# Six of the second layer's twelve modulation steps, moved from the first layer to the place between the layers

## The chip, the cores and the metric

The kernel runs on one core of one Trainium2 chip. The metric is device time in microseconds. A core has TensorE (PE, matmuls), VectorE (DVE), ScalarE (ACT), GpSimd (POOL) and SyncE (SP, which issues most DMAs); they run side by side and wait for each other by semaphores.

## The reference

Two layers of a hybrid backbone block on 512 latent and 256 context tokens, 1024 wide. What matters here is the modulation at the head of each layer and where its parts are used:

```
for l in range(DEPTH):
    sh1, sc1, g1, sh2, sc2, g2 = split(silu(c) @ w_mod[l] + b_mod[l], 6)
    modc = split(silu(c_ctx) @ w_mod[l] + b_mod[l], 6)
    h = modulate(rms_norm(x, norm1_g[l]), sh1, sc1)
    hc = modulate(rms_norm(xc, norm1_g[l]), modc[0], modc[1])
    p_* = split(h @ w_in[l]), and of hc likewise
    mixed = concat(pooling, GQA, hyena, MLA) @ w_out[l]
    x_new = x + g1 * mixed
    x = x_new + g2 * expert_choice_ffn(modulate(rms_norm(x_new, norm2_g[l]), sh2, sc2))
```

`c` and `c_ctx` don't depend on the tokens, so a layer's modulation can be computed at any time before its norm. The first two of the six parts are needed by the layer's first norm, the others from the output projection on.

## The kernel before, in words

The modulation of a layer (`modulation`, L354) is twelve steps of 512 columns. A step loads two weight halves of 1 MB (`wmod[l, j, kh]`) through `load` (L239) into the ring `ringt` of three slots, on SP's queue. It has 16 matmuls of 32x512 in four column groups side by side (L367), a copy on ScalarE (`part`, L371), four transposes (L375), and a sum and the bias on VectorE (L377, L378). After the twelfth step the table `modT` is transposed and written to memory (L381 to L384, `mrow`). It is a generator: each `yield` is a place where other work can be written in between.

The second layer's modulation is such a generator, `self.side` (L316), advanced by ticks while the first layer's projection (`project_in`) and its MLA attention are written. A scheduler then orders the instructions of each engine. So the steps lie on TensorE between other matmuls, and their weights in SP's queue between other loads.

The end of layer 0 is its mixture of experts, 16 experts whose weights of 1 MB come through the same SP queue; each expert's rows are scattered back to `xs` by GpSimd (L1601). Between the layers (`layer`, L666 to L676) the tables of layer 1 are loaded, `row_loads` (L733) loads six tiles of 128 token rows (`xrow`) from `xs`, which must wait for the last scatters, and `norm_rows` computes each row's scale: a square with its sum on ScalarE (L745), root and reciprocal (L725, L726), a diagonal matrix `diag` on VectorE (L749). Then layer 1 begins: `norm1` multiplies rows by `diag` (L763), which transposes and scales them, and splits the result into a high part on ScalarE (`hT`, L766) and a low part on VectorE and GpSimd (L769 to L773). The projection's first matmuls are those of L797. Its weights (`win`) also come through `ringt`.

Of the kernel before, what the change touches and what calls it, by code (L numbers as in the profile page):

```python
# [10 lines left out]
F32 = mybir.dt.float32  # L11
F32R = mybir.dt.float32r
U32 = mybir.dt.uint32
AF = mybir.ActivationFunctionType
# [13 lines left out]
GW = [sum(b - a for a, b in g) for g in GROUPS]  # L28
# [147 lines left out]

SLOTS = ([0, 1, 4, 2, 5, 3], 5, 4), ([0, 1, 2, 7, 8, 3, 4, 5, 6], 6, 4)
EARLY = 3, 9
LATE_STEPS = ((1, 0), (1, 2), (2, 0), (2, 2))

SCALE_BY = dict(g="vvpppv", m="vvpvpp")
# [24 lines left out]
class Block:  # L206
# [50 lines left out]
    def run(self):  # L257
        nc, I = self.nc, self.I
        c = self.const
        self.cst = c.tile([128, I["cst"].shape[1]], F32, name="cst")  # L260
        nc.sync.dma_start(self.cst, I["cst"])
        self.ident = self.cst[:, 0:128]
        self.sel16 = self.cst[:, 128:144]
        self.off = self.cst[:, 144:146]
        self.flip = [self.cst[:64, 146:274], self.cst[:32, 274:402]]
        self.half = self.cst[:, 402:404]
        self.tok = self.cst[:, 404:408]
        self.ones = c.tile([128, 1], F32, name="ones")
        nc.vector.memset(self.ones, 1.0)
        self.eps = c.tile([128, 1], F32, name="eps")  # L270
        nc.vector.memset(self.eps, EPS)
        d = self.dram
        self.xs = [d.tile([n, D], F32, name=f"xs{i}") for i, n in enumerate((SEQ, CTX))]
        self.xh = [d.tile([n, D], F32, name=f"xh{i}") for i, n in enumerate((SEQ, CTX))]
        self.spec = {(l, s): d.tile([2, 128, 2 if s == "l" else 1, 2, 2, 256], F32, name=f"spec{l}{s}")
                     for l in range(2) for s in ("l", "c") if (l, s) != (1, "c")}
        self.sqn = {k: c.tile([128, 4], F32, name=f"sqn{k[0]}{k[1]}") for k in self.spec}
        self.mrow = [d.tile([48, 2, 128], F32, name=f"mrow{l}") for l in range(2)]
        cT = c.tile([128, 8, 2], F32, name="cT")
        nc.sync.dma_start(cT, I["cT"].rearrange("p (k s) -> p k s", s=2))  # L280
        tables = self.open_layer(0)
        self.lay0 = self.lay
        self.scT = self.lay.tile([128, 8, 32], F32, name="scT")
        nc.vector.memset(self.scT, 0.0)
        nc.scalar.activation(self.scT[:, :, 0:2], cT, AF.Silu)
        self.small, self.modT = {}, {}
        self.load_small(0)
        npg, self.fcg = self.pool("norm"), self.pool("filtc")
        np_ = npg.__enter__()
        self.fc = self.fcg.__enter__()  # L290
        with self.pool("filt", side="right") as p:
            scr = dict(sp=[p.tile([128, 1024], F32, name=f"fsp{i}") for i in range(4)][::-1])
            self.filter_loads(p)
            self.filter_mlp(p, scr["sp"][3][:, :NT])
            p.tile([128, 2048], F32, name="spare")
            for k, w, n in (("od", 512, 2), ("acc", 1024, 1), ("s", 1024, 1)):
                scr[k] = [p.tile([128, w], F32, name=f"f{k}{i}") for i in range(n)]
            self.tabs["l"] = p.tile([128, 2, 2, 2, 256], F32, name="fdftl")
            scr["EO"] = [p.tile([128, 4096], F32, name="fEO")]
            scr["z"] = [self.fws]  # L300
            first = []
            for i in range(8):
                own = self.layt[:, 2048 * i - 6144:2048 * i - 4096] if i in (3, 4) else None
                first.append(self.load(I["wmod"][0, i // 2, i % 2], own=own))
                if i == 2:
                    nc.sync.dma_start(self.tabs["l"], I["fdftl"].rearrange("p (x r b f) -> p x r b f", x=2, r=2, b=2))
                if i == 4:
                    rows = self.row_loads(0, np_)
            mod = self.modulation(0, first)
            for _ in range(8):  # L310
                next(mod)
            for t, src in tables:
                nc.sync.dma_start(t, src)
            xh = self.norm_rows(np_, rows)
            self.filters(scr, "l")
        self.side = chain(mod, self.modulation(1))  # L316
        for l in range(DEPTH):
            npg, xh = self.layer(l, npg, xh) or (None, None)

# [31 lines left out]
        return self.small[l][:, a:b]  # L351


    def modulation(self, l, first=()):  # L354

        nc = self.nc
        if l not in self.small:
            self.load_small(l)
        mod = self.const.tile([128, 96], F32, name="modT", tag="modT", bufs=2)
        self.modT[l] = mod  # L360
        bm = self.sm(l, "b_mod")
        for j in range(12):
            pt = self.ps1()
            for kh in range(2):
                w = first.pop(0) if first else self.load(self.I["wmod"][l, j, kh])
                for kk in range(4):
                    nc.tensor.matmul(pt[32 * kk:32 * kk + 32, :], self.scT[:, 4 * kh + kk, :],  # L367
                                     w[:, 512 * kk:512 * kk + 512], start=kh == 0, stop=kh == 1,
                                     tile_position=(0, 32 * kk))
            part = self.lay0.tile([128, 512], F32, name="part", tag="part", bufs=1)  # L370
            nc.scalar.activation(part, pt, AF.Copy)  # L371
            yield
            pm = self.ps1()
            for q in range(4):
                nc.tensor.transpose(pm[:, 128 * q:128 * q + 128], part[:, 128 * q:128 * q + 128], self.ident)  # L375
            m = mod[:, 8 * j:8 * j + 8].rearrange("p (q s) -> p q s", s=2)
            nc.vector.tensor_reduce(m, pm.rearrange("p (q k s) -> p q s k", q=4, k=4)[:, :, 0:2], axis=AX.X, op=OP.add)  # L377
            nc.vector.tensor_tensor(m, m, bm[:, 4 * j:4 * j + 4][:, :, None].to_broadcast([128, 4, 2]), op=OP.add)  # L378
            yield
        pr = self.ps1()  # L380
        nc.tensor.transpose(pr[:96, :128], mod, self.ident)  # L381
        row = self.lay0.tile([96, 128], F32, name="mrow", tag="mrow", bufs=1)
        nc.vector.tensor_copy(row, pr[:96, :128])
        nc.gpsimd.dma_start(self.mrow[l].rearrange("n s d -> (n s) d"), row)  # L384
        self.dump(f"mod{l}", mod)
# [161 lines left out]
    def layer(self, l, npg, xh):  # L547
# [28 lines left out]
        with ExitStack() as rows_stack:  # L576
            cvg = self.pool("cv")
            with self.pool("hT", side="right") as hp:
                hT = [hp.tile([128, 8, NT], F32R, name=f"hT{i}") for i in range(2)]
                self.norm1(l, hT, xh, A1, B1)  # L580
                if not l:
                    g = self.G.rearrange("p b w -> p (b w)")
                    od = self.fc.tile([128, 512], F32, name="fod")
                    scr = {k: [self.fc.tile([128, w], F32, name="f" + k)] for k, w in (("s", 1024), ("sp", 1024), ("z", 512))}
                    self.filters(dict(scr, od=[od], EO=[g[:, 0:2048]], acc=[g[:, 2048:3072]]), "c")
                    self.fcg.__exit__(None, None, None)
                self.conv_tables(l, last)
                self.gain_tables(l)
                npg.__exit__(None, None, None)
                rows = rows_stack.enter_context(self.pool("rows"))  # L590
                self.MQ = rows.tile([128, 6, 384], F32, name="rowsMQ")
                self.MK = rows.tile([128, 6, 384], F32, name="rowsMK")
                self.MV = rows.tile([128, 6, 256], F32, name="rowsMV")
                self.rsq = rows.tile([128, 6, 12], F32, name="rsq")
                self.cv = cvg.__enter__().tile([128, 6, wid], F32, name="cv")
                self.project_in(l, hT, last, side)
# [70 lines left out]
        nxt = None  # L667
        if not last:
            tables = self.open_layer(l + 1)
            npg = self.pool("norm")  # L670
            np_ = npg.__enter__()
            rows = self.row_loads(l + 1, np_)
            for t, src in tables:
                nc.sync.dma_start(t, src)
            nxt = npg, self.norm_rows(np_, rows)
        r3g.__exit__(None, None, None)  # L676
        return nxt

# [75 lines left out]
    def norm1(self, l, hT, xh, A1, B1):  # L754
        nc, p = self.nc, self.npool
        for s, b0, nb in ((0, 0, 4), (1, 4, 2)):
            o = 128 * b0
            w = 128 * nb
            for k in range(8):
                pt = self.ps1()  # L760
                for i in range(nb):
                    x, d = xh[b0 + i]
# [12 lines left out]
    def project_in(self, l, hT, last, side):  # L775
# [3 lines left out]
        wp, rp = wpg.__enter__(), rpg.__enter__()  # L779

        def split_group(g):
            w = self.load(self.I[f"win{g}"][l], 8 * GW[g])
            n = GW[g]
            hi, lo = [], []
            for k in range(8):
# [919 lines left out]
```

## Time and profile before

| | us |
|---|---|
| median of 3 runs | 1486.69 (1483.56 to 1487.9) |
| the profiled execution's own time | 1484.3 |
| its span in the trace | 1482.4 |

The mean granted clock of TensorE over the span is 0.952 of full speed. Durations are read from the profiled execution, whose span is 1.9 us shorter than its time; rows are in microseconds from the span's start, mean durations in ns where a view says so. SPq is SP's issuing sequencer.

### The profile page before, as it was taken

What the parts mean: (1) busy time and instruction counts of PE and PEld (TensorE: products, weight loads), DVE (VectorE), ACT (ScalarE), POOL (GpSimd) and SP (SyncE); (2) the same over time, 40 slices, a digit from 0 to 9 for tenths busy, and PEclk for the clock granted to TensorE, in tenths of its full rate; (3) what the DMA queues carried; (4) which work ended last, traced back from release to release, by engine and by line L of the source; (5) the groups of instructions that cost most, each with busy time, mean ns of one, the idle gap of its engine ahead of it and who ended that gap; (6) DMA issues with size and microseconds to landing.
All of it is one profiled execution on the core that took longest, in us unless ns stands there. A gap on an engine that the chain in (4) does not pass through costs nothing.

```text
span 1482.4 us, 23909 instructions
## 1 busy us (share of the span) xinstructions
PE 1345.9 (91%) x9457; PEld 888.8 (60%) x9457; DVE 684.3 (46%) x1831; ACT 507.1 (34%) x1238; POOL 341.9 (23%) x360
## 2 busy tenths in 40 slices
PE   6999999888899998999999968988899974998896
PEld 2577787777678895444444437977778961332221
DVE  4656364687663547122222227585787452221111
ACT  4545333435564433111111136544357430111000
POOL 1510141254210115121222132042521011111101
PEclk9989999999899998999999989999999986999998
DMA  9546746011265139899999980123100858999996
GB/s 386 220 159 243 278 156 245 31 58 43 79 264 170 58 128 350 341 395 392 396 392 398 386 283 5 61 83 139 57 30 3 350 203 326 406 393 409 405 402 215
DMA packets 72737, 345.96 MB, mean 233 GB/s; under 512 B 7105, under 2 KB 23105, under 8 KB 38322
## 3 DMA queue, kind: packets, MB, share of 16 engines
q1 hardware_dynamic: 57488, 305.24, 52.3%
q0 software_dynamic: 13104, 32.19, 8.0%
q10 hardware_dynamic: 2034, 7.00, 1.2%
q8 instruction: 75, 1.23, 0.3%
q14 instruction: 36, 0.29, 0.1%
HBM read 317.70 MB, written 26.71 MB: 232 GB/s over the span
## 4 chain that ended last, share of the span: by engine, by line
PE 74%; DVE 9%; DMA 9%; ACT 3%; issue 3%; POOL 1%; POOLq 0%; ACTq 0%; DVEq 0%; SPq 0%
PE b L1622 13%; PE b L808 7%; PE b L1655 6%; PE b L1633 4%; PE b L1116 3%; PE b L367 3%; PE b L797 3%; PE b L798 3%; PE b L799 3%; PE b L1064 3%; DMA ring<-wu 3%; PE b L1304 3%; PE b L1306 3%; PE b L1305 3%; PE b L1139 3%
## 5 line engine op out<-in xcount | busy, mean ns | idle before, releaser
L1622 PE MATMUL b<-ring,xg 128*64 128x512 f32 x824 | 222.4, 618 | 13.5 <-DMA ring<-wu 10.6
L1622 PEld LDWEIGHTS b<-ring,xg 128*64 128x64 f32 x824 | 66.9, 141 | 130.5 <-issue 103.1
L1608 ACT ACTIVATE sgl<-b 64x512 f32<-64x512 f32 x32 | 18.9, 591 | 345.9 <-PE b L1622 345.9
L1655 PE MATMUL b<-ring,hTm 128*64 128x512 f32 x464 | 110.9, 605 | 2.0 <-DVE hTm L1649 1.3
L797 PE MATMUL b<-whi,hT 128*128 128x256 f32 (+1 forms) x352 | 103.1, 294 | 0.3 <-DVE h L769 0.3
L798 PE MATMUL b<-wlo,hT 128*128 128x256 f32 (+1 forms) x352 | 100.3, 285 | 0.0
L799 PE MATMUL b<-whi,hT 128*128 128x256 f32 (+1 forms) x352 | 99.9, 284 | 0.0
L1116 PE MATMUL b<-kop,qop 96*128 96x512 f32 (+3 forms) x360 | 86.1, 370 | 13.5 <-ACT P L1121 10.8
L808 PE MATMUL b<-hT,whi 128*128 128x512 f32 (+1 forms) x384 | 96.3, 357 | 1.5 <-DVE cv L864 1.3
L721 DVE TENSOR_TENSOR wlo<-ringt,whi 128x256 fp32r<-128x256 f32 (+1 forms) x192 | 83.0, 474 | 30.1 <-ACT whi L718 29.7
L1649 DVE COPY hTm<-b 128x384 f32<-128x384 f32 (+1 forms) x32 | 15.7, 491 | 164.0 <-PE b L1646 98.3
L718 ACT ACTIVATE whi<-ringt 128x256 fp32r<-128x256 f32 (+1 forms) x192 | 67.5, 404 | 47.6 <-PE b L808 22.4
L1601 POOL DMA_INDIRECT xs<-y,sidx x32 | 50.2, 1568 | 135.0 <-DVE y L1599 131.5
L1121 ACT ACTIVATE P<-b,nm 128x768 f32<-128x768 f32 (+1 forms) x80 | 65.4, 818 | 38.9 <-DVE nm L1118 37.2
L1118 DVE TENSOR_REDUCE nm<-b 128x1 f32<-128x768 f32 (+1 forms) x80 | 67.1, 845 | 23.1 <-PE b L1116 22.4
L797 PEld LDWEIGHTS b<-whi,hT 128*128 128x128 f32 x352 | 68.4, 195 | 12.3 <-issue 3.7
L1116 PEld LDWEIGHTS b<-kop,qop 96*128 96x128 f32 (+1 forms) x360 | 58.5, 201 | 25.2 <-ACT P L1121 14.0
L808 PEld LDWEIGHTS b<-hT,whi 128*128 128x128 f32 x384 | 63.2, 188 | 15.3 <-ACT oT L1263 2.1
L1304 PE MATMUL b<-whi,oT 128*128 128x256 f32 x240 | 71.3, 299 | 0.0
L798 PEld LDWEIGHTS b<-wlo,hT 128*128 128x128 f32 x352 | 68.7, 195 | 3.2 <-issue 2.5
L1655 PEld LDWEIGHTS b<-ring,hTm 128*64 128x64 f32 x464 | 32.7, 138 | 60.9 <-issue 57.4
L1144 ACT ACTIVATE PT<-b 128x384 f32<-128x384 f32 (+1 forms) x140 | 57.3, 448 | 34.4 <-PE b L1139 33.5
(398 smaller groups left out, 2881.1 us busy)
## 6 DMA issues: line engine op xcount, KB each, us to landing
ring<-wd SPq DMA_DIRECT2D x58, 1024.0 KB
ring<-wu SPq DMA_DIRECT2D x53, 1024.0 KB
ring<-wg SPq DMA_DIRECT2D x50, 1024.0 KB
ringt<-wmod SPq DMA_DIRECT2D x46, 1024.0 KB
ringt<-win SPq DMA_DIRECT2D x14, 1024.0 KB
ringt<-wg SPq DMA_DIRECT2D x14, 1024.0 KB
ringt<-wu SPq DMA_DIRECT2D x11, 1024.0 KB
ringt<-wout SPq DMA_DIRECT2D x8, 1024.0 KB
```

What stands on the lines that cost most here:

```text
L718: nc.scalar.activation(hi, src, AF.Copy)
L721: nc.vector.tensor_tensor(lo, src, hi.bitcast(F32), op=OP.subtract)
L797: nc.tensor.matmul(pt[:, :n], hT[0][:, k, t], hi[k], start=k == 0, stop=False)
L798: nc.tensor.matmul(pt[:, :n], hT[0][:, k, t], lo[k], start=False, stop=False)
L799: nc.tensor.matmul(pt[:, :n], hT[1][:, k, t], hi[k], start=False, stop=k == 7)
L808: nc.tensor.matmul(pt[:, a:b], w[k][:, cs], hT[h][:, k, a:b], start=first and k == 0, stop=end and k == 7)
L1116: nc.tensor.matmul(S[:, s:e], q[a][:K, c], k[b][:K, k0 + s:k0 + e], start=y == 0, stop=y == len(terms) - 1)
L1118: nc.vector.tensor_reduce(nm, S[:, :n], axis=AX.X, op=OP.max, negate=True)
L1121: nc.scalar.activation(P[:, :n], S[:, :n], AF.Exp, bias=nm, accum_out=sm)
L1304: nc.tensor.matmul(pt[:, :256], oT[0][k][:, t], hi[k], start=k == 0, stop=False)
L1622: nc.tensor.matmul(pa[64 * j:64 * j + 64], X[:, k, o:o + 64], w[k // 4][:, c], start=k == 0, stop=k == 7, tile_position=(0, 64 * j))
L1655: nc.tensor.matmul(py[64 * j:64 * j + 64], hT[:, f], wd[f // 2][:, d:d + 512], start=f == 0, stop=f == 3, tile_position=(0, 64 * j))
```

## The change

`SPLIT = 6`: the generator of layer 1 in layer 0 runs its steps 0 to 5 alone. A second one, for steps 6 to 11, is made between the layers, with a `scT` of its own (`scT1`, the activated `c`), a pool `wm` of three buffers and two slots of `ringt` for its twelve weight halves. The first projection weight (`win2`, `self.win0`) is loaded ahead of them. `in_order` makes TensorE keep the written order from there to the end of `norm1`. Steps 6 to 8 stand ahead of the norm, 9 to 11 in it. No arithmetic is added or left out.

```diff
-        self.side = chain(mod, self.modulation(1))
+        self.side = chain(mod, self.modulation(1, j1=SPLIT))
...
             tables = self.open_layer(l + 1)
-            npg = self.pool("norm")
+            npg, wmg = self.pool("norm"), self.pool("wm")
             np_ = npg.__enter__()
-            rows = self.row_loads(l + 1, np_)
+            scT = np_.tile([128, 8, 32], F32, name="scT1")
+            nc.gpsimd.memset(scT, 0.0)
+            nc.scalar.activation(scT[:, :, 0:2], self.cT, AF.Silu)
+            slots = [("wm", 3)] * 12
+            slots[3] = slots[4] = ("ringt", self.RING)
+            wm, todo = wmg.__enter__(), [(j, h) for j in range(SPLIT, 12) for h in range(2)]
+            ready = []
+
+            def fetch(n=1):
+                for _ in range(n):
+                    if todo:
+                        j, h = todo.pop(0)
+                        tag, bufs = slots.pop(0)
+                        w = (wm if tag == "wm" else self.ring).tile([128, 2048], F32, name=tag, tag=tag, bufs=bufs)
+                        nc.sync.dma_start(w, I["wmod"][l + 1, j, h])
+                        ready.append(w)
+
+            def take():
+                if not ready:
+                    fetch()
+                return ready.pop(0)
+
+            self.win0 = self.load(I["win2"][l + 1], 8 * GW[2])
+            fetch(5)
+            mod = self.modulation(l + 1, [take] * 12, SPLIT, 12, np_, scT)
             for t, src in tables:
                 nc.sync.dma_start(t, src)
+            self.between = self.in_order()
+            self.between.__enter__()
+            next(mod)
+            fetch(2)
+            next(mod)
+            next(mod)
+            rows = self.row_loads(l + 1, np_)
+            fetch(1)
+            next(mod)
+            next(mod)
             nxt = npg, self.norm_rows(np_, rows)
+            next(mod)
+            self.late_mod = mod, fetch, wmg
...
             for k in range(8):
+                if l and (k in (1, 2, 4, 5) if not s else k in (1, 2)):
+                    next(self.late_mod[0], None)
+                    if k in (1, 4):
+                        self.late_mod[1](2)
                 pt = self.ps1()
```

On SP, the issues between layer 0's last expert weight (`ring<-wd`) and layer 1's projection weights, before:

```order
L1556 DMA ring_7921<-wd 128x2048
L239 DMA ringt<-win 128x1280
L239 DMA ringt<-win 128x2048 x2
L733 DMA xrow<-xs_75 128x1024 x4
L733 DMA xrow<-xs_76 128x1024 x2
L239 DMA ringt<-win 128x2048 x5
```

and in the changed kernel, at the same place:

```order
L1608 DMA ring_7784<-wd 128x2048
L241 DMA ringt<-win 128x1280
L698 DMA ringt<-wmod 128x2048 x2
L698 DMA wm<-wmod 128x2048 x6
L241 DMA ringt<-win 128x2048 x2
L698 DMA wm<-wmod 128x2048
L781 DMA xrow<-xs_75 128x1024 x4
L781 DMA xrow<-xs_76 128x1024 x2
L241 DMA ringt<-win 128x2048
L698 DMA wm<-wmod 128x2048 x3
L241 DMA ringt<-win 128x2048 x4
```

Nine `wmod` loads now stand ahead of the token rows `xrow`, and three behind them.

On TensorE, the same place: the last expert's final matmuls (`hTm`) and the beginning of layer 1's norm (`diag,xrow`), before:

```order
L1663 MATMUL b_8188<-ring_7919,hTm 32x256 x8
L1663 MATMUL b_8188<-ring_7921,hTm 32x256 x8
L763 MATMUL b_8306<-diag,xrow 128x128
L763 MATMUL b_8315<-diag,xrow 128x128
L763 MATMUL b_8324<-diag,xrow 128x128
L763 MATMUL b_8333<-diag,xrow 128x128
L763 MATMUL b_8306<-diag,xrow 128x128
```

and in the changed kernel (`wm,scT` and `ringt,scT` are a step's matmuls, `cst,part` its transposes):

```order
L1715 MATMUL b_8051<-ring_7784,hTm 32x256 x8
L372 MATMUL b_8106<-wm,scT_8084 32x512 x8
L380 MATMUL b_8121<-cst,part 128x128 x4
L372 MATMUL b_8128<-wm,scT_8084 32x512 x4
L372 MATMUL b_8128<-ringt,scT_8084 32x512 x4
L380 MATMUL b_8153<-cst,part 128x128 x4
L372 MATMUL b_8160<-ringt,scT_8084 32x512 x4
L372 MATMUL b_8160<-wm,scT_8084 32x512 x4
L380 MATMUL b_8219<-cst,part 128x128 x4
L815 MATMUL b_8247<-diag,xrow 128x128 x4
L372 MATMUL b_8256<-wm,scT_8084 32x512 x8
L815 MATMUL b_8271<-diag,xrow 128x128 x4
```

Steps 6 to 8 stand ahead of the norm, step 9 behind its first group of columns. The norm's groups are now written one after the other, where before the first four were filled row by row. (One matmul of a step in the program is two in the trace: x8 here is its 16 there.)

## Rows read from the trace of the kernel before

**Rows 1.** The page, part 4: the chain that ended last, share of the span by engine.
```profile
PE 74%; DVE 9%; DMA 9%; ACT 3%; issue 3%; POOL 1%; POOLq 0%; ACTq 0%; DVEq 0%; SPq 0%
```

**Rows 2.** The chain in 238 to 264: start, us, what.
```profile
249.25 0.44 PE b L375 x4
249.68 1.85 PE b L367 x16
```

**Rows 3.** The lines of 400 to 456: busy us, mean ns, idle before.
```profile
L371 ACT ACTIVATE part<-b 128x512 f32<-128x512 f32 x5 | 3.0, 597 | 4.5 <-PE b L367 4.5
```

**Rows 4.** The chain in 398 to 457: start, us, what.
```profile
400.60 1.85 PE b L367 x16
...
406.62 0.59 PE b L375 x4
...
434.92 1.00 PE b L367 x8
...
437.51 0.99 PE b L367 x8
...
456.30 0.26 PE b L381
456.58 0.30 DVE mrow L383
```

**Rows 5.** Windows: us, busy of PE, PEld, DVE, ACT, POOL; clock, DMA share, GB/s.
```profile
410.00:420.00 10.00, 9.64 (x104) 7.33 (x102) 5.82 (x15) 7.82 (x21) 0.48 (x1) 1.00 0.47 173
440.00:450.00 10.00, 10.00 (x95) 7.54 (x94) 5.84 (x14) 7.34 (x19) 1.81 (x2) 1.00 0.43 140
1120.00:1130.00 10.00, 10.00 (x98) 8.79 (x97) 7.50 (x16) 8.38 (x22) 1.21 (x2) 1.00 0.01 2
```

**Rows 6.** TensorE's waits in 384 to 456: us in total, times, longest.
```profile
PE b L1139 <- ACT PT L1144: 0.4, 1, 0.4
```

**Rows 7.** Windows between the layers, columns as in rows 5.
```profile
844.00:852.00 8.00, 8.00 (x61) 2.97 (x59) 1.70 (x8) 0.00 (x0) 3.10 (x2) 1.00 1.01 409
...
862.00:866.00 4.00, 3.30 (x44) 1.61 (x42) 1.79 (x3) 0.34 (x1) 3.84 (x15) 1.00 1.02 428
866.00:870.00 4.00, 4.00 (x32) 1.55 (x32) 0.66 (x1) 0.00 (x0) 2.73 (x2) 1.00 0.77 146
870.00:874.00 4.00, 1.17 (x24) 0.42 (x16) 2.54 (x10) 1.69 (x7) 2.48 (x2) 1.00 0.49 44
...
878.00:882.00 4.00, 0.00 (x0) 0.00 (x0) 0.00 (x0) 1.78 (x3) 0.00 (x0) 0.50 0.94 347
882.00:886.00 4.00, 2.41 (x11) 2.44 (x12) 1.14 (x6) 3.92 (x9) 0.00 (x0) 0.50 1.03 406
886.00:892.00 6.00, 4.37 (x25) 4.17 (x24) 2.69 (x8) 5.94 (x12) 0.00 (x0) 0.73 0.42 173
892.00:898.00 6.00, 4.96 (x40) 4.44 (x39) 6.00 (x11) 4.29 (x8) 3.93 (x3) 1.00 0.00 0
898.00:904.00 6.00, 4.18 (x28) 3.48 (x29) 6.00 (x12) 3.52 (x7) 3.21 (x4) 1.00 0.00 0
```

**Rows 8.** SP's rows in 850 to 890: first issue, us, what.
```profile
857.29 2.05 SPq L239 DMA_DIRECT2D ringt<-win  x3
876.25 3.08 SPq L733 DMA_DIRECT2D xrow<-xs  x6
```

**Rows 9.** ScalarE's rows in 868 to 904: start, us, what.
```profile
880.20 1.06 ACT L745 ACTIVATE junk<-xrow 128x1024 f32<-128x1024 f32 x1 [8.39 <-issue]
...
889.44 2.78 ACT L766 ACTIVATE hT<-b,B,A 128x512 fp32r<-128x512 f32 x4
```

**Rows 10.** TensorE's rows in 868 to 904.
```profile
883.59 6.48 PE L763 MATMUL b<-diag,xrow 128*128 128x128 f32 x32 [12.42 <-DVE diag L749]
...
903.50 0.34 PE L797 MATMUL b<-whi,hT 128*128 128x160 f32 x1 [0.26 <-DVE h L769]
```

**Rows 11.** The line of a step's matmuls: duration in ns, min/median/max.
```profile
L367 PE MATMUL b<-ringt,scT x368: 592/592/1062, 12.2 to 448.0; 128*32 128x512 f32 x184
```

More of the change, by code (lines that the diff above doesn't have):

```diff
@@ L178 @@
 EARLY = 3, 9
+SPLIT = 6
 LATE_STEPS = ((1, 0), (1, 2), (2, 0), (2, 2))
@@ L278, in run @@
         self.mrow = [d.tile([48, 2, 128], F32, name=f"mrow{l}") for l in range(2)]
-        cT = c.tile([128, 8, 2], F32, name="cT")
+        cT = self.cT = c.tile([128, 8, 2], F32, name="cT")
         nc.sync.dma_start(cT, I["cT"].rearrange("p (k s) -> p k s", s=2))
@@ L351, in sm, with modulation @@
         return self.small[l][:, a:b]
-    def modulation(self, l, first=()):
+    def modulation(self, l, first=(), j0=0, j1=12, p=None, scT=None):
         nc = self.nc
@@ L358, in modulation @@
             self.load_small(l)
-        mod = self.const.tile([128, 96], F32, name="modT", tag="modT", bufs=2)
-        self.modT[l] = mod
+        if not j0:
+            self.modT[l] = self.const.tile([128, 96], F32, name="modT", tag="modT", bufs=2)
+        mod = self.modT[l]
         bm = self.sm(l, "b_mod")
-        for j in range(12):
+        p, scT = p or self.lay0, self.scT if scT is None else scT
+        for j in range(j0, j1):
             pt = self.ps1()
@@ L365, in modulation @@
                 w = first.pop(0) if first else self.load(self.I["wmod"][l, j, kh])
+                w = w() if callable(w) else w
                 for kk in range(4):
-                    nc.tensor.matmul(pt[32 * kk:32 * kk + 32, :], self.scT[:, 4 * kh + kk, :],
+                    nc.tensor.matmul(pt[32 * kk:32 * kk + 32, :], scT[:, 4 * kh + kk, :],
                                      w[:, 512 * kk:512 * kk + 512], start=kh == 0, stop=kh == 1,
                                      tile_position=(0, 32 * kk))
-            part = self.lay0.tile([128, 512], F32, name="part", tag="part", bufs=1)
+            part = p.tile([128, 512], F32, name="part", tag="part", bufs=1)
             nc.scalar.activation(part, pt, AF.Copy)
@@ L379, in modulation @@
             yield
+        if j1 < 12:
+            return
         pr = self.ps1()
         nc.tensor.transpose(pr[:96, :128], mod, self.ident)
-        row = self.lay0.tile([96, 128], F32, name="mrow", tag="mrow", bufs=1)
+        row = p.tile([96, 128], F32, name="mrow", tag="mrow", bufs=1)
         nc.vector.tensor_copy(row, pr[:96, :128])
@@ L580, in layer @@
                 self.norm1(l, hT, xh, A1, B1)
+                if l:
+                    for _ in self.late_mod[0]:
+                        pass
+                    self.between.__exit__(None, None, None)
+                    self.late_mod[2].__exit__(None, None, None)
                 if not l:
@@ L781, in split_group @@
         def split_group(g):
-            w = self.load(self.I[f"win{g}"][l], 8 * GW[g])
+            w = self.win0 if l and g == 2 else self.load(self.I[f"win{g}"][l], 8 * GW[g])
             n = GW[g]
```

## The prediction

> **What bounds the kernel now.** I read five views in order: the chain that ended last, the stretches in which the six moved steps run, TensorE's waits there, the stretch between the layers, and the rows of DMA issues, ScalarE and TensorE in it. The chain is TensorE's for 74% of the span [rows 1], so TensorE time taken off is a gain wherever TensorE has no gaps, and time put where TensorE waits costs nothing by itself.
>
> The moved steps first. Only one of the six lies beside the first layer's projection: its 16 matmuls start at 249.68 [rows 2]. The other five lie in the MLA attention of layer 0: five ScalarE copies, one for each step, in 400 to 456 [rows 3]. In that attention TensorE is busy 9.64 and 10.00 us of 10, at full clock [rows 5], and it waits 0.4 us in 72 [rows 6]. The reader is to see that the weights are always there and that ScalarE (7.82 of 10) and VectorE (5.84) have room: what leaves TensorE here comes off the end. Layer 1's same attention, which has no modulation in it, also stands at 10.00 of 10 with ScalarE at 8.38 [rows 5], so I expect the thinned attention to stay with TensorE.
>
> Between the layers it is the other way. After the last expert TensorE waits 12.4 us for the first `diag` [rows 10]. Until 866 the expert weights and the projection's first weights come at 409 to 428 GB/s [rows 7]; then the queue is nearly empty, because the six token rows (`xrow`) are issued only at 876.25, after the last expert's scatters [rows 8]. The first row reaches ScalarE at 880.20 [rows 9], the norm's matmuls run from 883.59 and the projection begins at 903.50 [rows 10]. In that norm ScalarE is busy 5.94 of 6 us from 886 to 892, and VectorE 6.00 of 6 from 892 to 904 [rows 7]: it is a chain over three engines, and TensorE has gaps in it.
>
> **The gain in layer 0.** Per step the chain has 16 matmuls, 1.85 us, and four transposes, 0.59 us [rows 4]. The five steps in the attention: four times 1.85, once 1.00 + 0.99 (in two halves), and five times 0.59: 9.39 + 2.95 = 12.3 us. After the last one stand the transposition of the whole table, 0.26, and the copy on which the attention then waits, 0.30: 0.6 us [rows 4]. The projection's step is 1.85 us and 0.44 us of transposes (taken from those of the step ahead of it) [rows 2]: 2.3 us. Sum 15.2 us. I take 15.0, since single gaps may reopen. The lower bound is 12: it lets a fifth be lost to ScalarE and VectorE, which have 2 to 4 us of every 10 left. The twelve weight loads that leave layer 0's queue count nothing: TensorE waited for no weight there [rows 6].
>
> **The price between the layers.** Steps 6 to 8 stand before the norm, where TensorE has 12.4 us of nothing to do, so their matmuls are hidden by that wait, and so are the memset and the activation that rebuild `scT`: ScalarE is idle in 844 to 852 [rows 7]. What isn't hidden is their weights. In SP's order nine of the twelve 1 MB loads stand before `xrow`, and the projection's `win` loads with them, as now. The three loads that were issued at 857.29 [rows 8] keep the queue busy until about 867.4 (146 GB/s over 866 to 870 is 1.4 us at 428 [rows 7]). After the change two `wmod` loads stand at the place of two of these, and what follows is nine loads more: 9 x 1.049 MB at 409 GB/s is 23.1 us, to 890.5. The first row, 0.52 MB, is then in at 891.8. Before, 3.95 us passed from its issue to ScalarE's start (876.25 to 880.20), 1.3 of them transfer; the issue now lies behind the queue, and I leave 0.8 for the receipt: 892.6 instead of 880.2, **12.4 us later**. At 428 GB/s it would be 10.5; at the 347 of 878 to 882 [rows 7] it would be 16.5. Behind `xrow` on SP stand one `win` load, the last three `wmod` loads and the other `win` loads; the first two projection groups have theirs by then.
>
> Next, three steps stand inside the norm. They are 3 x (1.85 + 0.59) = 7.3 us of TensorE. [...] So I double the first: 2.4 us more, 9.8 in all. In 886 to 904 TensorE has 1.6 + 1.0 + 1.8 = 4.4 us free [rows 7]. If these gaps take the work, 5.3 us remain, **which I add**. The lower bound is the three ScalarE copies alone, 1.8 us; the upper is 9.8, nothing hidden. TensorE's order also turns from row by row to group by group: the first group now needs four rows' `diag`. Its copy to `hT` came only after all six rows' squares anyway (889.44 [rows 9]), so I count nothing for it.
>
> [...]
>
> **The sum**: -15.0 + 12.4 + 5.3 = +2.7 us on the profiled execution's 1484.3: 1487.0. That execution stands 2.4 under the runs' median of 1486.7, so I name **1489.4 us**. A measurement of this kernel tells about 0.3%, 4.5 us, from no change.
>
> **The rivals.**
> A. My forecast, with its own range from the bounds that lie together: 1484 to 1494. Chance 0.45.
> B. Slower: the norm is stretched by whole steps. The last three loads are issued only when step 9 frees their buffers, behind the rows; each norm group behind a waiting step waits too, since TensorE keeps the written order. Then the inserted steps cost 9.8 instead of 5.3, and one late load of 2.6 us shows: +9.8 in all, 1496. For it: TensorE's order is strict, and ScalarE is at 5.94 of 6. Against it: the norm lasts 20 us, in which three loads are 7.7. It decides as soon as the inserted steps cost over 7.1. Chance 0.33.
> C. Faster: the rows aren't held by the queue. They can be issued when step 8 has freed its buffer: its weights are the fourth of the nine loads, in at 867.4 + 4 x 2.56 = 877.6, so near 878.5, 2.3 later than now. If their packets then pass the `wmod` loads that are queued, the price is 2.3 + 5.3 = 7.6 and the time -7.4: 1479. For it: the rows are 3.1 MB of the 15 that are in the queue. Against it: the loads issued at 857.29 were still in the queue at 867, so what is issued next stands behind ten us of work now, too. Chance 0.14.
> D. Layer 0 gives back only part: the attention is then held by its softmax chain, and half of the 12.3 us is lost: +8.9, 1496. For it: of every 10 us 7.8 would be left to TensorE (12.3 of some 56 are gone), and 7.2 to ScalarE (7.82 less a copy of 0.6). Against it: layer 1's attention [rows 5]. Chance 0.08.
>
> [...]
>
> **How the numbers follow.** A's own range crosses 4.5 us either way a little: of its 0.45, 0.38 is within, 0.05 above, 0.02 below. B gives 0.28 slower and 0.05 within, C 0.12 faster and 0.02 within, D 0.08 slower. So faster 0.14, same 0.45, slower 0.41. The range 1480 to 1499 holds A, B and D's midpoint and leaves out most of C and the far ends: about 2 in 10.
>
> **What would show it.** In the changed profile: no row of the step in 400 to 440 and an attention about 12 us shorter; DMA near full share from 862 to 895 of the present time scale where it is now 0.49 at 870 to 874; ScalarE's first square about 12 us later, counted from the last expert matmul; the time from the first norm matmul to the projection 4 to 8 us longer than 19.9. I am wrong if the first square is less than 5 us later, if the norm takes over 28 us, or if the attention stays as long as it is.

## The result, and the profile after

The changed kernel takes 1502.2 us (median of 7 runs, 1492.1 to 1505.5) against 1485.3 (7 runs): the ratio is 1.010, 95% interval 1.0074 to 1.0127. It is slower, by about three times what a measurement tells from no change, and above the range that was given. The profiled execution took 1503.0 us, its span 1501.1.

TensorE's share of the chain fell and DMA's rose, against [rows 1]. The page's part 4 after the change:

```profile
PE 71%; DMA 13%; DVE 9%; ACT 4%; issue 2%; POOL 1%; POOLq 0%; ACTq 0%; SPq 0%; DVEq 0%
```

In the attention of layer 0 the steps are gone and TensorE is as full as in [rows 5], with ScalarE a little fuller. Windows after, columns as there:

```profile
400.00:410.00 10.00, 10.00 (x76) 8.60 (x77) 7.60 (x18) 8.05 (x23) 1.82 (x2) 1.00 0.01 2
440.00:450.00 10.00, 10.00 (x118) 8.53 (x118) 5.16 (x15) 8.00 (x28) 2.66 (x7) 1.00 0.18 54
```

Between the layers, TensorE's rows after, which answer to [rows 10]. The last expert's matmuls end at 863.88:

```profile
863.90 1.06 PE L372 MATMUL b<-wm,scT 128*32 128x512 f32 x8
867.47 1.53 PE L372 MATMUL b<-wm,scT 128*32 128x512 f32 x8 [2.50 <-DMA wm<-wmod]
...
878.52 0.65 PE L380 MATMUL b<-cst,part 128*128 128x128 f32 x4 [0.78 <-ACT part L376]
892.55 0.77 PE L815 MATMUL b<-diag,xrow 128*128 128x128 f32 x2 [13.38 <-DVE diag L797]
...
897.25 3.64 PE L372 MATMUL b<-wm,scT 128*32 128x512 f32 x16
...
904.72 1.92 PE L372 MATMUL b<-wm,scT 128*32 128x512 f32 x16
...
911.22 1.92 PE L372 MATMUL b<-wm,scT 128*32 128x512 f32 x16
...
918.74 0.34 PE L849 MATMUL b<-whi,hT 128*128 128x160 f32 x1
```

Steps 6 to 8 end at 879.2 and TensorE then waits 13.4 us, a little longer than the 12.4 without them: the gap was not filled, it was moved behind the steps. Why is seen in the chain of the same stretch (start, us, what), where two DMA pieces take 21 us of the 62 from 857 to 919:

```profile
857.21 10.21 DMA wm<-wmod
...
878.19 10.81 DMA xrow<-xs
889.10 1.15 ACT junk L793 x2
```

and in the windows, which answer to [rows 7]: the queue is full throughout, and in the middle it moves 357 GB/s, not 409.

```profile
854.00:864.00 10.00, 9.28 (x96) 3.86 (x96) 2.59 (x5) 0.00 (x0) 6.68 (x17) 1.00 1.02 412
864.00:878.00 14.00, 9.77 (x56) 2.45 (x55) 1.39 (x7) 1.32 (x3) 3.13 (x2) 0.76 1.05 357
878.00:890.00 12.00, 0.65 (x4) 0.42 (x4) 2.24 (x10) 3.17 (x10) 0.00 (x0) 0.65 1.02 413
```

**Stage by stage.** I cut each trace at the first or last matmul of a stage: the end of the projection (L808), the last hyena matmul (L1218), the first of the router (L1339), the first and the last of the experts (L1622, L1663), the first and last of the norm (L763), and the same in layer 1. The first column is before, in us; the others are differences to it in the profile of each kernel (the experiments are told below).

| stage | before | changed | e5 | e1 | e2 | e3 | e4 | e6 | e7 | e8 | e9 | e10 |
|---|---|---|---|---|---|---|---|---|---|---|---|---|
| layer 0 hyena, first attention | 102.7 | +5.4 | +3.5 | +1.9 | +0.4 | +0.4 | +3.5 | +4.3 | +3.4 | 0.0 | +3.5 | -0.2 |
| to the attention's end | 80.8 | -14.2 | -12.6 | -14.2 | -1.7 | -14.2 | -12.6 | -14.2 | -12.6 | -7.7 | -12.6 | -12.6 |
| output projection, routing | 133.8 | +2.4 | +4.4 | +4.1 | -0.2 | +3.9 | +4.4 | +4.2 | +4.4 | +9.9 | +4.4 | +4.1 |
| experts | 276.7 | +0.3 | -0.9 | -0.9 | +0.4 | -0.9 | -0.9 | -0.9 | -0.9 | -0.5 | -0.9 | -0.9 |
| wait for the norm | 12.4 | +16.3 | +16.3 | -0.9 | +16.7 | +16.2 | +12.8 | +15.7 | +4.5 | +9.4 | -1.7 | -1.1 |
| norm | 19.7 | +6.1 | +6.5 | -1.0 | +5.9 | +6.0 | +9.2 | 0.0 | +1.8 | -0.8 | -1.0 | -0.8 |
| layer 1 projection | 122.4 | +1.6 | 0.0 | -1.4 | 0.0 | +1.6 | 0.0 | -1.4 | +2.4 | 0.0 | +0.4 | -0.5 |
| layer 1 hyena, first attention | 64.0 | +4.3 | +4.4 | -1.0 | +2.5 | -2.0 | +2.5 | -1.0 | +0.3 | +0.7 | +7.7 | +9.0 |
| to the attention's end | 64.5 | -0.6 | -0.6 | 0.0 | -0.7 | 0.0 | -0.6 | 0.0 | +0.2 | 0.0 | +6.1 | +2.7 |

Ahead of the first stage the code is that of before, but for the projection's step where SPLIT is 6, and it ends between 272.5 and 282.1 us in these profiles (276.3 on average in the seven without that step, 279.1 in the five with it). A step of 2.3 us can't be read from such a spread. Nor do differences of about 1 us in a stage mean much: from the experts to layer 1's hyena e1 runs the work of before, and its stages are 0.9 to 1.4 shorter than in the one profile of before, whose 1484.3 us stand 3 above the later medians of before (1481.3 and 1481.5). So the ratios are the measure of a kernel, the stages that of a place.

### The profile page after: what moved, and what is told of

Its sections match the earlier page's. It is cut to its first block, busy times and chain, and to the rows that moved or that the text cites. A ratio compares the mean times of both kernels' runs of the same rounds, so it can differ in the third digit from the quotient of the medians.

```text
span 1501.1 us, 23922 instructions
## 1 busy us (share of the span) xinstructions
PE 1347.3 (90%) x9457; PEld 890.7 (59%) x9457; DVE 679.9 (45%) x1831; ACT 507.8 (34%) x1239; POOL 342.1 (23%) x361
## 4 chain that ended last, share of the span: by engine, by line
PE 71%; DMA 13%; DVE 9%; ACT 4%; issue 2%; POOL 1%; POOLq 0%; ACTq 0%; SPq 0%; DVEq 0%
PE b L1674 11%; PE b L860 7%; PE b L1707 5%; PE b L1685 4%; DMA ring<-wg 4%; DMA ring<-wu 4%; PE b L1168 3%; PE b L1116 3%; PE b L849 3%; PE b L1191 3%; PE b L372 3%; PE b L850 3%; PE b L851 3%; PE b L1356 2%; PE b L1357 2%; PE b L1358 2%
## 5 line engine op out<-in xcount | busy, mean ns | idle before, releaser
L1674 PE MATMUL b<-ring,xg 128*64 128x512 f32 x824 | 216.4, 600 | 16.2 <-DMA ring<-wu 12.3
L1168 PE MATMUL b<-kop,qop 96*128 96x512 f32 (+3 forms) x360 | 84.8, 365 | 13.1 <-ACT P L1173 10.5
L1701 DVE COPY hTm<-b 128x384 f32<-128x384 f32 (+1 forms) x32 | 15.7, 490 | 159.1 <-PE b L1698 98.2
L849 PEld LDWEIGHTS b<-whi,hT 128*128 128x128 f32 x352 | 68.3, 195 | 12.2 <-issue 3.7
L860 PEld LDWEIGHTS b<-hT,whi 128*128 128x128 f32 x384 | 63.9, 190 | 14.3 <-issue 2.7
L1168 PEld LDWEIGHTS b<-kop,qop 96*128 96x128 f32 (+1 forms) x360 | 57.8, 198 | 22.8 <-ACT P L1173 13.6
L851 PEld LDWEIGHTS b<-whi,hT 128*128 128x128 f32 x352 | 68.5, 195 | 0.8 <-issue 0.8
```

What stands on the lines that cost most here:

```text
L849: nc.tensor.matmul(pt[:, :n], hT[0][:, k, t], hi[k], start=k == 0, stop=False)
L851: nc.tensor.matmul(pt[:, :n], hT[1][:, k, t], hi[k], start=False, stop=k == 7)
L860: nc.tensor.matmul(pt[:, a:b], w[k][:, cs], hT[h][:, k, a:b], start=first and k == 0, stop=end and k == 7)
L1168: nc.tensor.matmul(S[:, s:e], q[a][:K, c], k[b][:K, k0 + s:k0 + e], start=y == 0, stop=y == len(terms) - 1)
L1674: nc.tensor.matmul(pa[64 * j:64 * j + 64], X[:, k, o:o + 64], w[k // 4][:, c], start=k == 0, stop=k == 7, tile_position=(0, 64 * j))
```

## The experiments

**e1: the layer 0 part alone.** Against the changed kernel:

```diff
         if j1 < 12:
-            return
+            nc.gpsimd.memset(mod[:, 8 * j1:], 0.0)
...
-            scT = np_.tile([128, 8, 32], F32, name="scT1")
...
             self.win0 = self.load(I["win2"][l + 1], 8 * GW[2])
-            fetch(5)
-            mod = self.modulation(l + 1, [take] * 12, SPLIT, 12, np_, scT)
+            rows = self.row_loads(l + 1, np_)
...
```

> Steps 6 to 11 are left out altogether (their columns of the table are zeros), so this is the layer 0 part of the change alone. Forecast: TensorE's time comes off the end, 13 to 15 us faster than before, near 1471. Rival 1, the attention can't use the time that is freed: 9 to 10 us faster, near 1476, as the changed kernel's layer 0 gave. Rival 2, the changed kernel's layer 0 lost some 5 us because the scheduler wrote the hyena stage in another order: here that order is nearly the one of before, so 13 to 15 us faster as well, and the stretch from the projection to the end of the hyena is as long as before within 2 us.

Measured: ratio 0.9936 (0.9923 to 0.9949), 9.5 us. The 13 to 15 that were expected did not come: the amount is rival 1's, but not the place. The attention itself gives the whole 14.2: TensorE waits 0.2 us in 400 to 448, so rival D is out, and so is rival 1 as it was put. But 4.1 us are given back in the routing and 1.9 in the hyena, whose order here is neither that of before nor that of the changed kernel.

**e2: the price alone.**

```diff
-        self.side = chain(mod, self.modulation(1, j1=SPLIT))
+        self.side = chain(mod, self.modulation(1, end=False))
...
-        if j1 < 12:
+        if not end:
             return
```

> Layer 0 computes all twelve steps as before, and steps 6 to 11 are computed once more between the layers (work is added): the price of the new place alone. Forecast: 17.7 us slower than before, near 1503. Rival, the queue is slower than its best rate and the rest of layer 1 is written in another order too: 22 us between the layers and some 4 to 5 behind them, near 1511.

Measured: 1.0184 (1.0167 to 1.0201), 27.3 us, near what the rival expected (22 and some 4 to 5) and not the 17.7. In the profile 16.7 + 5.9 of it lie between the layers and 2.5 in layer 1's hyena. e1 and e2 together give +1.2%, the changed kernel's +1.0 to +1.2%: the two parts add up.

**e6 and e7: loads without steps, steps without loads.** The price is split once more.

```diff
-                for kk in range(4):
+                for kk in range(0 if dry else 4):
...
+            if dry:
+                yield
+                yield
+                continue
```
```diff
-                        w = (wm if tag == "wm" else self.ring).tile([128, 2048], F32, name=tag, tag=tag, bufs=bufs)
-                        nc.sync.dma_start(w, I["wmod"][l + 1, j, h])
-                        ready.append(w)
+                        if (j, h) == (SPLIT, 0):
+                            one.append(wm.tile([128, 2048], F32, name="wm", tag="wm", bufs=3))
+                            nc.sync.dma_start(one[0], I["wmod"][l + 1, j, h])
+                        ready.append(one[0])
```

> Between the layers the nine weight loads that stand ahead of the token rows are issued as in the changed kernel, but steps 6 to 11 are left out (no matmul, copy or transpose; their columns of the table are zeros). If the queue makes the rows late: the first norm matmul is 27 to 29 us after the last expert's (28.7 in the changed kernel, 12.4 before) and the norm is as long as before (19.7, plus or minus 1). If the steps' work on TensorE makes the wait: the first norm matmul comes after 13 to 16 us.

> Steps 6 to 11 are computed at the new place with all their matmuls, but all from one weight half, loaded once: eleven of the twelve loads are left out, so the steps' values are not those of the reference. If the queue makes the rows late: the first norm matmul comes 12 to 15 us after the last expert's, the norm stays 5 to 6 us longer than before, and the time is some 15 us less than the changed kernel's. If the steps make the wait: 20 us or more to the first norm matmul.

Measured: e6 1.0056 (1.0033 to 1.0080), e7 1.0017 (0.9999 to 1.0035). In e6, whose last expert matmul ends at 863.90, ScalarE's first square and TensorE's first norm matmul:

```profile
888.65 1.06 ACT L798 ACTIVATE junk<-xrow 128x1024 f32<-128x1024 f32 x1 [24.10 <-DMA xrow<-xs]
```
```profile
892.04 0.76 PE L820 MATMUL b<-diag,xrow 128*128 128x128 f32 x2 [28.14 <-DVE diag L802]
```

and TensorE's rows in e7, where the last expert matmuls end at 865.34,

```profile
865.43 1.92 PE L372 MATMUL b<-wm,scT 128*32 128x512 f32 x16
...
881.37 1.11 PE L380 MATMUL b<-cst,part 128*128 128x128 f32 x4 [7.51 <-ACT part L376]
882.28 1.96 PE L816 MATMUL b<-diag,xrow 128*128 128x128 f32 x8
```

with ScalarE's, the first square and step 8's copy:

```profile
875.68 1.06 ACT L794 ACTIVATE junk<-xrow 128x1024 f32<-128x1024 f32 x1 [4.38 <-DMA xrow<-xs]
...
880.74 0.57 ACT L376 ACTIVATE part<-b 128x512 f32<-128x512 f32 x1
```

Nine loads with no work on them make TensorE wait 28.1 us; six steps with one load let the norm begin after 16.9. The loads alone cost 15.7 (wait +15.7, norm 0), the steps alone 6.3 (wait +4.5, norm +1.8). The sum, 22.0, is that of the changed kernel, 22.4. But e7's wait came out 2 over its expectation and its norm 3 to 4 under, for a reason of its own: step 8's copy stands behind three of the rows' squares on ScalarE, so TensorE waits 7.5 us for it (in the changed kernel the copy runs at 877.87, 11 us ahead of the first square). Counted from the first square the split is plainer. The first square comes 9.0 us after the last expert matmul before, 25.2 in the changed kernel, 24.8 in e6 and 10.3 in e7; from there to the projection it takes 23.3, 29.6, 23.8 and 28.5. So the loads make the rows late, and the steps make the norm 5 to 6 us longer.

**e4: the rows on a queue of their own.**

```diff
-                self.nc.sync.dma_start(x, self.xsrc(l)[s][128 * b:128 * b + 128])
+                (self.nc.gpsimd if l else self.nc.sync).dma_start(x, self.xsrc(l)[s][128 * b:128 * b + 128])
```

> The changed kernel with the six token rows of layer 1 issued by GpSimd, on its own queue, behind its last scatters, instead of by SP behind nine weight loads. If the place in SP's queue makes the rows late: the first square comes 5 to 10 us earlier against the last expert matmul than in the changed kernel (25.2 there, 9.0 before), and the time is 5 to 8 us less than the changed kernel's. If it is the bandwidth, shared by whatever is in flight: the rows come as late as before this edit, and the time is within 2 us of the changed kernel's.

Measured: 1.0143 (1.0128 to 1.0157), so no faster than the changed kernel. Neither expectation fits as it was put: the first square comes 3.5 us earlier, and nothing is won by it. On GpSimd's queue, too, the rows are issued late:

```profile
884.00 2.21 POOL L781 DMA_DIRECT2D xrow<-xs  x4 [4.34 <-DMA xs<-y,sidx]
```

That is 13.7 us after the last expert matmul (870.34), when the scatters that they read from have landed; in the changed kernel SP issues them after 14.3,

```profile
878.19 4.89 SPq L781 DMA_DIRECT2D xrow<-xs  x6
```

and before after 5.1. Beside the weight loads a scatter takes twice as long from issue to landing (us, the last ones, before and in e4; in the changed kernel 8.7; in e7, with one load, 4.1 to 4.7):

```profile
DMA to landing us min/median/max: 4.2/4.6/5.0
DMA to landing us min/median/max: 8.8/9.2/9.6
```

The first square comes 8.0 us after the issue, in the changed kernel 10.9, but the other rows trickle in. TensorE's rows in e4, one for each of the first four row tiles:

```profile
895.57 0.77 PE L815 MATMUL b<-diag,xrow 128*128 128x128 f32 x2 [10.49 <-DVE diag L797]
897.93 0.80 PE L815 MATMUL b<-diag,xrow 128*128 128x128 f32 x2 [1.59 <-DVE diag L797]
901.69 0.79 PE L815 MATMUL b<-diag,xrow 128*128 128x128 f32 x2 [2.97 <-DVE diag L797]
903.70 0.80 PE L815 MATMUL b<-diag,xrow 128*128 128x128 f32 x2 [1.21 <-DVE diag L797]
```

They stand 2.4, 3.8 and 2.0 us apart (in the changed kernel the rows' first matmuls stand 1.3 to 1.4 apart). Wait and norm together are 22.0 longer than before, against 22.4. The last row's square comes 34.9 us after the last expert matmul, in the changed kernel 34.2, before 17.2. So off SP's queue the first row is 3.5 us earlier and the last 0.7 later. With the weights in flight the scatters are late (8.8 to 9.6 us, before 4.2 to 5.0), and the rows as a whole on either queue.

**e5: the changed kernel once more.** No edit.

> The changed kernel once more, on one chip with the next three, because its times spread over 13 us where those of before spread over 4. If the spread is a matter of single executions: a median 15 to 17 us above before. If the stages that differ (hyena of layer 0 +5.4, routing +2.4, hyena of layer 1 +4.3, between the layers +22.5) belong to the program: the same four stages are longer by the same amounts within 1 us in this profile; if they belong to the execution, one or more of them is back at before's length.

Measured: 1.0118 (1.0091 to 1.0145). All four stages are longer again: hyena +3.5 (it was +5.4), routing +4.4 (+2.4), between the layers +22.8, layer 1's hyena +4.4. They belong to the program, but two of them vary by 2 us, not by the 1 that was expected.

**e3, and e8: five and three steps instead of six.**

```diff
-SPLIT = 6
+SPLIT = 7
```
```diff
-SPLIT = 6
+SPLIT = 9
```

> SPLIT is 7: five steps move instead of six, the one beside the projection stays. Nine of the ten loads still stand ahead of the token rows, two steps in the norm instead of three. The order of the hyena stage is, in both layers, that of the kernel before. If the reordering costs the changed kernel some 10 us (6 in layer 0, 4 in layer 1): 7 to 10 us faster than the changed kernel although less is taken off layer 0, near 1493. If reordering costs nothing and the loss is the queue's and the norm's: within 3 us of the changed kernel, near 1500.

> SPLIT is 9: three steps move, all ahead of the norm, with six loads instead of nine ahead of the rows. If each load costs what the changed profile shows (32 us for eleven, 2.9 each) beyond a slack of 9.9 us that the queue had: the first norm matmul comes 7.5 us later than before, the norm is as long as before, layer 0 gives 7, and the time is that of before within 2 us. By the forecast's 2.56 us for each load: 4.7 us later, and 3 us faster than before.

Measured: e3 1.0108 (1.0086 to 1.0129), within the changed kernel's interval. The 7 to 10 us did not come, so by its expectation the run speaks for the other side: reordering costs nothing in the whole time. Yet its hyena stages are back, +0.4 and -2.0 against e5's +3.5 and +4.4. Against e5's profile these are 9.5 us, but what lies ahead of the first stage ends 7.2 later (the step that stays is 2.3 of it; whether the rest is chance isn't known), and the ratios differ by 0.1%. The stages are shorter; that the whole is shorter by it isn't shown. What TensorE waits for in layer 0's hyena (us in total, times, longest), in the changed kernel:

```profile
PE b L1270 <- DVE layt L1263: 8.1, 3, 3.9
PE b L1270 <- DVE hyscr L1263: 7.6, 3, 4.7
PE b L1168 <- ACT P L1173: 4.2, 2, 2.9
PE b L1247 <- DVE hyscr L1253: 2.9, 1, 2.9
```

and in e3:

```profile
PE b L1270 <- DVE hyscr L1263: 7.8, 3, 4.7
PE b L1168 <- ACT P L1173: 6.9, 4, 4.4
PE b L1270 <- DVE layt L1263: 3.9, 2, 3.7
```

In the changed order TensorE waits 4.2 us longer for `layt` and 2.9 for a `hyscr` that it didn't wait for, and 2.7 less for the softmax (`P`).

e8: 1.0048 (1.0026 to 1.0070), 7 us slower instead of equal. Six loads cost 9.4 us of wait, more than both expectations (7.5 and 4.7); the three steps hidden ahead of the norm cost it nothing. Its profile is its longest execution (1499.6, median 1490.1) and fell on a long routing stage (+9.9).

**e9 and e10: another place.** Steps 6 to 11 (e10: 7 to 11) beside layer 1's hyena, nothing between the layers.

```diff
+                if last:
+                    wmp = wmg.__enter__()
...
+                    side.add(self.modulation(l, ws, SPLIT, 12, wmp, scT))
...
             step(self.attend(p, "g", 0, i, *ops["g", 0]))
+            if last:
+                side.tick(2)
```

> A third place for the six steps: in layer 1, beside its hyena and first attention, where TensorE has 12 us of gaps and the queue is nearly empty (30 to 60 GB/s), with two weight buffers of their own; nothing between the layers. Layer 0 gives what it gave alone, 9 to 10 us. If the gaps take half of the steps' 14.6 us: 2 to 3 us faster than before, near 1479. If the hyena's chain over three engines is stretched by work in its gaps: as much is lost in layer 1 as layer 0 gives, or more, within 2 us of before or slower. Between the layers the stretch is as long as before, plus or minus 1 us, in both cases.

> The same with SPLIT at 7: the step beside the projection of layer 0 stays, and the hyena of layer 0 keeps the order of the kernel before. If that reordering costs 3 to 5 us: 1 to 3 us faster than the run with SPLIT at 6, although one step less leaves layer 0 (2.3) and one less comes to layer 1. If reordering costs nothing: the same time within 1 us, and the stretch from the projection to the hyena's end is no shorter.

Measured: e9 1.0034 (1.0012 to 1.0055), e10 0.9985 (0.9961 to 1.0009): e10 is as fast as before, and neither beats it. The norm's wait is back at 10.8 and 11.3. But layer 1's hyena and attention grow by 13.8 and 11.7 us, nearly all of what the steps take (14.6 and 12.2), though TensorE had 12 us of gaps there. The steps did not fall into the gaps: in layer 1's hyena TensorE is busy 51.88 us of 64.02 before and 62.13 of 73.04 in e10, so 10.9 us still stand open.

```profile
1025.87:1089.89 64.02, 51.88 (x340) 45.30 (x340) 53.77 (x92) 27.29 (x59) 30.66 (x26) 0.89 0.10 34
1012.72:1085.76 73.04, 62.13 (x423) 48.91 (x423) 55.62 (x104) 31.03 (x66) 31.55 (x26) 0.93 0.47 173
```

e10 beats e9 by half a percent, 7 us, more than the 1 to 3 expected. The order of layer 0's hyena accounts for 3.6 us in the table; the 2.1 by which layer 1 grows less is about the step that stays in layer 0 (2.3). The two profiled executions don't show it as a whole: e9's (1482.6) lies below its median (1486.8), e10's (1482.3) above its own (1479.8).

## Why the prediction was wrong

**Right.** The attention gave what was summed for it: 14.2 us (12.6 in e5) where the five steps and the table's end came to 12.9. Steps 6 to 8 were hidden, and the norm grew by 6.1 us where 5.3 were added. The clock had fallen again when it began (0.65 in 878 to 890): step 9's 16 matmuls took 3.64 us, the later steps' 1.92. The forecast doubled a whole step for this, 2.4 us, its author's estimate: no run shows that figure, the matmuls took 1.7 longer, and before, the longest single one takes 1.8 times the median [rows 11]. The first square came 16.2 us later, counted from the last expert matmul (889.10 - 863.88 = 25.2 against 9.0): the mechanism forecast, its size at the upper bound.

**The step that failed first: the gain.** "Sum 15.2 us. I take 15.0, since single gaps may reopen." From the projection's end to the experts' start 12.9 of it should have come off, and 6.5 did, in e5 4.8. Nothing was costed for the rest of layer 0, nor for layer 1 behind its norm, which grew by 5.3 us (1.6 + 4.3 - 0.6; in e5 3.8). Two things go with it.

The first is the order in which the scheduler writes the hyena stage. When the step beside the projection goes, it is another one, and the stage is longer by 3.4 to 5.4 us in the six profiles with the new order (changed, e4, e5, e6, e7, e9) and by -0.2 to +1.9 in the five without it (e2, e3, e8 and e10 with the order of before; e1, where that step is gone too, with a third order and the +1.9). In layer 1 it is 2.5 to 4.4 in the four with a new order (changed, e2, e4, e5) and -2.0 to +0.7 in the five others without steps there. The forecast read the two places where the change acts, and not what a scheduler does with the rest. That the order is the cause is supported by its going with the length in eleven profiles and by e10 beside e9; no run changed the order alone, and e3 as a whole is no faster. So the order as the cause is argued, not shown.

The second is TensorE's clock in the routing: the stage is longer by 2.4 to 4.4 us in every run whose layer 0 is shortened (e8's +9.9 holds other waits too), and by -0.2 in e2, whose layer 0 isn't. TensorE has the same matmuls and nearly the same idle time there (5.6 us before, 5.8 in e1), but is busy longer at a lower mean clock. Before, and in e1:

```profile
460.70:594.50 133.80, 128.21 (x874) 107.50 (x873) 74.11 (x231) 48.79 (x123) 34.10 (x33) 0.95 0.50 180
447.50:585.40 137.90, 132.11 (x876) 110.60 (x875) 73.24 (x231) 48.82 (x123) 35.77 (x35) 0.93 0.50 184
```

In the last 11.6 to 16.2 us of that stage the granted clock was 0.86 before and 0.85 in e2, and 0.68 to 0.78 in the changed kernel, e1 and e3 to e7. Windows of 2 us at the end of that stage, before:

```profile
585.00:587.00 2.00, 1.33 (x6) 1.33 (x7) 1.89 (x6) 0.53 (x2) 1.97 (x3) 0.60 0.95 303
587.00:589.00 2.00, 2.00 (x12) 2.00 (x12) 0.82 (x2) 1.50 (x3) 1.70 (x2) 0.54 0.91 356
589.00:591.00 2.00, 2.00 (x20) 2.00 (x20) 0.00 (x0) 0.62 (x1) 0.17 (x1) 1.00 1.04 428
```

and in e5:

```profile
572.20:574.20 2.00, 2.00 (x10) 1.69 (x9) 1.25 (x8) 0.00 (x0) 0.00 (x0) 0.50 1.05 377
574.20:576.20 2.00, 1.49 (x6) 1.25 (x6) 1.20 (x4) 0.91 (x2) 1.56 (x2) 0.50 0.92 270
576.20:578.20 2.00, 2.00 (x11) 2.00 (x11) 1.30 (x4) 0.59 (x2) 1.95 (x2) 0.50 1.03 426
578.20:580.20 2.00, 2.00 (x11) 2.00 (x11) 0.41 (x1) 1.61 (x2) 0.76 (x1) 0.50 1.01 424
580.20:582.20 2.00, 2.00 (x12) 2.00 (x12) 0.00 (x0) 0.00 (x0) 0.00 (x0) 0.56 1.02 414
```

Before, the clock is near 0.50 in two of these windows (0.60 and 0.54), under 4 us; in e5 in all five (0.50 to 0.56), nearly ten us. TensorE's rows there, before:

```profile
580.25 1.84 PE L543 MATMUL b<-ones,ring 128*128 128x1 f32 x16
...
585.67 8.90 PE L1533 MATMUL b<-onehot,xn 128*128 128x128 f32 x64 [0.80 <-DVE onehot L1521]
```

and in e5:

```profile
569.12 1.84 PE L550 MATMUL b<-ones,ring 128*128 128x1 f32 x16
...
575.88 10.29 PE L1585 MATMUL b<-onehot,xn 128*128 128x128 f32 x64 [0.51 <-DVE onehot L1573]
```

The engine ran matmuls one column wide ahead of the fall in both, from 580.25 and 569.12 (the last window of 2 us at a clock of 1.00 ends at 585.00 and 570.20); the gather's 64 matmuls take 1.4 us more in e5, and others of the stage the rest. Why the clock falls earlier there stays open.

**The step that failed second: the queue's size.** The forecast had nine loads at 409 GB/s, 23.1 us, 12.4 of them showing; the first square came 16.2 later. That is within the bounds of 10.5 to 16.5 (with the 0.8 of receipt that the sum has and that no run shows by itself, they come to 11.3 and 16.7). What the sum put at nothing is the scatters' own time on the DMA engines. From the last expert matmul to the first square, 25.2 us, the changed profile has by queue (packets, MB, share of 16 engines):

```profile
q1 hardware_dynamic: 1395, 8.92, 87.5%
q0 software_dynamic: 530, 0.69, 15.9%
```

The scatters are those of q0, and 15.9% of 25.2 us is 4.0, about the 3.8 that the forecast lacks; before, the last of them ran while the other queue was empty: in 870 to 876 all 322 packets are q0's, at 62.9% of the engines' time. No run took the scatters away, so this is a sum and not a test. e6 shows that it takes no step for this wait: with the loads alone it is 28.1 us.

**The rivals.** B and D named the right side and the nearest time (1496), but not the cause. B's norm cost 6.1, not 9.8, and no step in it waited for its weights. C's first condition failed: the rows were to be issued 2.3 us later than before and were issued 9.2 later, counted from the last expert matmul (14.3 against 5.1). Its second, that they pass the weights, was not shown: on a queue of their own in e4 the first square came 3.5 us earlier and the last 0.7 later, and nothing is won. D's mechanism fell by e1, its amount (half of the gain lost) did not: the half went elsewhere. The sum in the changed profile, stage by stage: -14.2 + 5.4 + 2.4 + 0.3 + 16.3 + 6.1 + 1.6 + 4.3 - 0.6 is +21.6; the projection of layer 0 takes off 1.1, and behind layer 1's attention 1.7 more are taken off: but for rounding, the 18.7 by which the spans differ.

## What to carry to other kernels

Before an engine's gap is filled, ask what it waits for, and whether the new work's data comes by the same way. Here the gap was the wait for scatters and rows on DMA engines that moved 44 GB/s [rows 7], and the weights filled them: six loads made the gap 9.4 us longer (e8), nine made it 15.7 longer without any work on them (e6). Where a scheduler orders the program, compare the order and the length of the stages that a change doesn't touch too.

## What was not expected of the hardware

Full DMA share wasn't one rate in the changed kernel: 357 GB/s in 864 to 878, where the scatters' queue had 25.1% of the engines' time, 412 and 413 in the stretches ahead and behind, where it had 5.5 and 3.8%, all at a share of 1.02 to 1.05. The scatters are slower too: 8.8 to 9.6 us from issue to landing in e4, 4.2 to 5.0 before. And the same routing work took 2.4 to 4.4 us more in nine profiles with a shorter layer 0 than in the two without (before and e2), at a granted clock near its end of 0.68 to 0.78 in seven of them, against 0.86 and 0.85; why is open.
